# Embedding operand requested before the last group of ff1, two of four weight sums done by accumulating DMAs, another first and last stage

## The chip, the core and the metric

The kernel runs on one core of one Trainium2 chip. A core has a matrix engine (TensorE, here PE, with its weight loads as PEld), three elementwise engines (VectorE or DVE, ScalarE or ACT, GpSimd or POOL), a sync engine (SP), and 16 DMA engines that the queues of SP, ACT and POOL feed. The engines run their own instruction streams in order and wait for one another through semaphores. The metric is the device time of one execution in microseconds (us).

## The reference

A trunk of two layers on x of 512 frames by 1024 features, float32. Each layer has three parts, and a last norm follows:

```python
h  = rmsnorm(x, g1);  z = h @ W_in + b_in        # mLSTM q k v o i f, retention q k v g, two gates
x += (sig(gA) * (A @ W_bA) + sig(gB) * (B @ W_bB)) @ W_out    # A: mLSTM, B: retention, chunks of 64
x += relu(rmsnorm(x, g2) @ W1 + b1)**2 @ W2 + b2              # ff1 to 4096 features, ff2 back
x += sigmoid(rmsnorm(x, g3) @ W_pg) * (p[i] @ W_pe)           # per-layer embedding, p of 256 features
# after the last layer: out = rmsnorm(x, gf)
```

## The kernel before, in words

**Layout.** Everything is feature-major: x is a tile of 128 partitions x 8 tiles of features x 512 frames. Products are of float32 accuracy, made of three matmuls in the engine's rounded format (fp32r): each operand is split into a high part and the rest, and a product is hi·hi + hi·lo + lo·hi (`mm3`, lines 296 to 298; in pairs 338 to 340). ACT writes the high part (line 231), DVE subtracts it for the low one (line 232).

**Weights** come as blocks of 128 x 1024 (512 KB) in the order of use (`wstream`). `fill_raws` (line 250) keeps up to four raw blocks on their way on SP's queue; `prep_next` takes the next block, splits it into `wh` and `wl`; `ready(k)` prepares all up to the k-th piece, two units ahead of their use (`LOOK`). A T8 unit is one block for 24 matmuls over 512 columns. IF is the first unit of a layer (the mLSTM's gates, tile `l0if`).

**Norms.** `Norm.operand` writes gain times x, split (`l0n1h` on ACT, line 390; `l0n1l` on DVE, line 391); `square` makes the squares (ACT line 403, POOL line 401) and sums them over the feature tiles on POOL (line 409), all but the last one, which stays apart (`tail`). `finish` sums over partitions on PE with a matrix of ones, two matmuls for each 128 frames (`ss`, lines 416 and 417), POOL takes the root (`rc`), and `spread` puts the result on all partitions (`rp`, lines 434 and 435; `rb`, line 437). The scale is applied only behind the next matmul, so operands need not wait for it.

**ff1 and ff2.** Unit f(b,p) is two T8 tiles, evacuated and split into the hidden tiles `hh`, `hl`. ff2 is computed in groups of four pairs o(b,p), p = 0 to 3, by one level of the Winograd form of Strassen's product: 7 products of 12 matmuls over 256 columns instead of 8. Pair (b,p) adds into tiles 2p and 2p+1 of x on DVE (line 950). Its weights are four pieces out of two blocks r1 and r2: B11, t1 (a sum in r1), t2 (in r2) and t3 (a tile `t`), four half-block additions on DVE in all (lines 269, 270, 273, 277). The order of work is f(0,0..3), then for b = 0 to 2: f(b+1,0), o(b,0..3), f(b+1,1..3); then the matmuls of p[i] @ W_pe (two units PE, operand `pth`/`ptl` from `pT`, result `l0pe`), then the last group o(3,0..3), in which the tiles of the third norm (`n3.tile`) are made as x becomes final; then the gate tiles `pg` with n3's `finish` and `spread`.

**Tail.** The last four gate tiles are computed in halves of 256 frames, so that the last norm has two halves, n40 and n41; `final` multiplies x by gain and scale (three tiles on POOL, line 1050, five on DVE, line 1052) and sends it out (line 1054).

**What sets the order.** The code is written in program order, but the framework's scheduler decides at build time the order of instructions on each engine; on the chip each engine runs its own list in order. Names below are those of the first layer with l0, of the second with l1.

Of the kernel before, what the change touches and what calls it, by code (L numbers as in the profile page):

```python
# [33 lines left out]
F32 = mybir.dt.float32  # L34
# [15 lines left out]
LOOK = 2  # L50
RAWS = 4
PIECES = 3
PAD = 16
# [129 lines left out]
def build(ctx, tc, ins, out):  # L183
# [52 lines left out]
    for n, u in enumerate(units):  # L236
        if u[0] == "PAIR":
            order += [(n, x) for x in PIECE]
            loads += [(n, 0), (n, 1)]
        else:  # L240
            order.append((n, 0))
            loads.append((n, 0))
    place = {x: k for k, x in enumerate(order)}
# [3 lines left out]
    def fill_raws(most=RAWS):  # L247
        while at["load"] < len(loads) and sum(k[1] != "t" for k in raws) < most:
            raws[loads[at["load"]]] = r = wpool.tile([P, UN], F32, name=f"wr{at['load']}", tag="wr", bufs=RAWS)
            nc.sync.dma_start(r, ins["wstream"][at["load"]])  # L250
            at["load"] += 1

    def prep_next():
# [7 lines left out]
        if x in PIECE:  # L261
# [3 lines left out]
            if x == "B11":  # L265
                src, out_ = r2[:, c0], piece(cur["xw"], "b", Q)
            elif x == "t1":
                raws[n, "t"] = t = cur["xw"].tile([P, UN], F32, name=f"t{n}", tag="t")
                ve.tensor_tensor(t[:, c0], r1[:, c0], r2[:, c1], OP.add)
                ve.tensor_tensor(r1[:, c0], r1[:, c0], r2[:, c0], OP.add)  # L270
# [98 lines left out]
    class Norm:  # L369
# [23 lines left out]
        def square(self, k, x, pool=False):  # L393
            w = self.n * P
            x = x[:, self.s]
            if self.sum is None:
                sq = opool.tile([P, T], F32, name=f"{self.name}sum", tag="ssum" + self.half)[:, :w]
# [6 lines left out]
            if self.sum is None:  # L404
                self.sum = sq
            elif k == KT - 1:
                self.tail = sq
# [3 lines left out]
        def finish(self):  # L411
            n = self.name
            o = ps(f"{n}ss")
            for j in range(self.n):
                s = slice(j * P, (j + 1) * P)
                te.matmul(o[:, 2 * j:2 * j + 2], self.sum[:, s], ones[:, 0:2], start=True, stop=False)
                te.matmul(o[:, 2 * j:2 * j + 2], self.tail[:, s], ones[:, 0:2], start=False, stop=True)
# [6 lines left out]
        def spread(self):  # L424
# [11 lines left out]
            self.b = opool.tile([P, T], F32, name=f"{n}rb", tag="rb" + self.half)[:, :w]  # L436
# [175 lines left out]
    fill_raws(2)  # L612
    for k in range(0, KT, 2):
        nc.sync.dma_start(x[:, k:k + 2, :], ins["xT"][k:k + 2].rearrange("k p t -> p k t"))
    for k in range(KT):
        n1.operand(k, x[:, k, :])
    fill_raws()
    for k in range(KT):
        n1.square(k, x[:, k, :], k < 5)
# [3 lines left out]
    for i in range(L):  # L623
# [30 lines left out]
        for k in range(KT):  # L654
            s = slice(k * P, (k + 1) * P)
            mm3(og, wh[:, s], wl[:, s], xa[0][k], xa[1][k], k == 0, k == KT - 1)

# [280 lines left out]

        def ff2(b, p):
            def make(n):  # L940
# [11 lines left out]
                def done(x_, o):  # L952
# [8 lines left out]
                    elif x_ == "P4":  # L961
                        add(0, o, OP.add)
                        if b == 3:
                            for c in (2 * p, 2 * p + 1):
                                n3.tile(c, x[:, c, :])
# [7 lines left out]
        for kind, b, p in first:  # L973
# [3 lines left out]
            if group:  # L977
                run_pairs(group)
                group = []
# [208 lines left out]
```

## Time and profile before

| | us |
|---|---|
| three runs | 2444.41, 2439.2, 2441.95 |
| median | 2441.95 |
| profiled execution | 2438.42 |
| its span, first to last instruction | 2436.7 |
| mean granted TensorE clock | 0.993 |

The page's instruction count is 30731. The rows of a timeline read: start, duration, engine, line, operation, output <- inputs, shapes, number, and in brackets the engine's idle time before it and what ended it. In a list of waits, a row is the waiting instruction <- what it waited for: us in total, times, longest. A row that groups instructions gives shortest/median/longest in ns and the first and last start. A row of DMA issues gives queue, number, size and the median us from issue to landing.

In 40 equal slices of the span, the page has PE in tenths busy and the DMA engines' throughput:

```profile
PE   8999999999999999998999999999999999999997
...
GB/s 165 93 89 77 83 104 87 86 85 132 78 121 130 113 104 87 104 113 72 132 90 89 91 83 95 95 95 82 92 120 87 122 134 90 113 104 96 95 87 44
```

PE is at nine tenths or more nearly throughout, and lower at both ends.

### The profile page before, as it was taken

To read this page: it belongs to the slowest core of one execution; us is meant where nothing else is said; L and a number is where in the kernel's file an instruction comes from. 1 tells how busy PE (TensorE), PEld (TensorE's weight loads), DVE (VectorE), ACT (ScalarE), POOL (GpSimd) and SP (SyncE) were. 2 spreads that over 40 slices of the span, in tenths; PEclk is the share of its full clock that TensorE was granted. 3 is DMA by queue.
4 is the path that set the end of the run, shared out by engine and by line. 5 is a ranking of instruction groups with operands and counts; after the bars stand their busy time and mean duration, and the time that the engine had idled before them with its cause. 6 is when DMAs were issued, how large, how long until landed. Compare 5 with 4: busy or idle time off the path is not lost.

```text
span 2436.7 us, 30731 instructions
## 1 busy us (share of the span) xinstructions
PE 2390.5 (98%) x12220; PEld 2040.2 (84%) x12220; DVE 1574.1 (65%) x2403; ACT 1042.2 (43%) x1420; POOL 142.1 (6%) x213
## 2 busy tenths in 40 slices
PE   8999999999999999998999999999999999999997
PEld 6888888888888899898888888888888888998786
DVE  7867536663555678777778665466635547788675
ACT  4746323332333545544446552233333335445443
POOL 4100000000001000000201000000000010000012
PEclk9999999999999999999999999999999999999998
DMA  4222232223234332332322222222232342332221
GB/s 165 93 89 77 83 104 87 86 85 132 78 121 130 113 104 87 104 113 72 132 90 89 91 83 95 95 95 82 92 120 87 122 134 90 113 104 96 95 87 44
DMA packets 74417, 241.41 MB, mean 99 GB/s; under 512 B 8089, under 2 KB 10521, under 8 KB 74273
## 3 DMA queue, kind: packets, MB, share of 16 engines
q1 hardware_dynamic: 64336, 221.49, 27.3%
q10 hardware_dynamic: 9936, 17.96, 2.4%
q8 instruction: 96, 1.57, 0.3%
q14 instruction: 49, 0.39, 0.0%
HBM read 231.02 MB, written 8.39 MB: 98 GB/s over the span
## 4 chain that ended last, share of the span: by engine, by line
PE 95%; DVE 3%; ACT 1%; issue 1%; POOL 0%; DVEq 0%; ACTq 0%; POOLq 0%
PE l0f L296 2%; PE l1f L296 2%; PE l1f L297 2%; PE l0f L297 2%; PE l0f L298 2%; PE l1f L298 2%; PE l1br L297 1%; PE l1br L296 1%; PE l0br L298 1%; PE l0br L297 1%; PE l0br L296 1%; PE l1br L298 1%; PE l1bgm L296 1%; PE l0bgm L296 1%; PE l0wo L297 1%
## 5 line engine op out<-in xcount | busy, mean ns | idle before, releaser
L231 ACT ACTIVATE wh<-wr 128x1024 fp32r<-128x1024 f32 x342 | 361.7, 1059 | 851.8 <-issue 161.4
L232 DVE TENSOR_TENSOR wl<-wr,wh 128x1024 fp32r<-128x1024 f32 x342 | 419.1, 1227 | 216.0 <-ACT wh L231 215.7
L231 ACT ACTIVATE wh_t<-wr 128x1024 fp32r<-128x1024 f32 x64 | 66.9, 1058 | 84.6 <-DVE wr L270 53.6
L296 PE MATMUL l0f<-l0n2h,wh 128*128 128x512 f32 x256 | 99.8, 390 | 0.0
L296 PE MATMUL l1f<-l1n2h,wh 128*128 128x512 f32 x256 | 99.8, 390 | 0.0
L298 PE MATMUL l1f<-l1n2h,wl 128*128 128x512 f32 x256 | 99.7, 389 | 0.0
L298 PE MATMUL l0f<-l0n2h,wl 128*128 128x512 f32 x256 | 99.7, 389 | 0.0
L297 PE MATMUL l1f<-l1n2l,wh 128*128 128x512 f32 x256 | 99.7, 389 | 0.0
L297 PE MATMUL l0f<-l0n2l,wh 128*128 128x512 f32 x256 | 99.6, 389 | 0.0
L232 DVE TENSOR_TENSOR wl_t<-wr,wh_t 128x1024 fp32r<-128x1024 f32 x64 | 77.1, 1218 | 19.4 <-ACT wh_t L231 19.2
L231 ACT ACTIVATE wh_t<-t 128x1024 fp32r<-128x1024 f32 x32 | 33.9, 1061 | 58.6 <-DVE t L277 14.2
L298 PEld LDWEIGHTS l0f<-l0n2h,wl 128*128 128x128 f32 x256 | 48.1, 188 | 10.2
L298 PEld LDWEIGHTS l1f<-l1n2h,wl 128*128 128x128 f32 x256 | 48.1, 188 | 10.1
L297 PEld LDWEIGHTS l0f<-l0n2l,wh 128*128 128x128 f32 x256 | 48.1, 188 | 9.8
L297 PEld LDWEIGHTS l1f<-l1n2l,wh 128*128 128x128 f32 x256 | 48.1, 188 | 9.7
L296 PEld LDWEIGHTS l1f<-l1n2h,wh 128*128 128x128 f32 x256 | 48.1, 188 | 9.7
L296 PEld LDWEIGHTS l0f<-l0n2h,wh 128*128 128x128 f32 x256 | 48.1, 188 | 9.6
L232 DVE TENSOR_TENSOR wl_t<-t,wh_t 128x1024 fp32r<-128x1024 f32 x32 | 39.1, 1222 | 7.6 <-ACT wh_t L231 7.6
L231 ACT ACTIVATE wh_B<-wr 128x512 fp32r<-128x512 f32 x32 | 20.0, 626 | 24.6 <-issue 8.8
L409 POOL TENSOR_TENSOR l0n3sum<-l0n3sum,l0n3sq 128x512 f32<-128x512 f32 x6 | 9.4, 1572 | 348.9 <-issue 319.3
L409 POOL TENSOR_TENSOR l1n3sum<-l1n3sum,l1n3sq 128x512 f32<-128x512 f32 x6 | 8.9, 1487 | 349.3 <-ACT l1n3sum L403 319.7
L297 PE MATMUL l0pg<-l0n3l,wh 128*128 128x512 f32 x64 | 25.0, 393 | 0.2 <-DVE l0n3l L391 0.2
(3117 smaller groups left out, 7581.7 us busy)
## 6 DMA issues: line engine op xcount, KB each, us to landing
wr<-wstream SPq DMA_DIRECT2D x406, 512.0 KB, 3.3
x<-xT SPq DMA_DIRECT2D x4, 512.0 KB, 7.2
br_spill<-l0brs ACTq DMA_DIRECT2D x8, 256.0 KB, 2.0
l0brl<-br_spill ACTq DMA_DIRECT2D x8, 256.0 KB, 2.7
l0xr<-xT ACTq DMA_DIRECT2D x8, 256.0 KB, 2.7
x_spill<-l0x ACTq DMA_DIRECT2D x8, 256.0 KB, 2.2
br_spill<-l1brs ACTq DMA_DIRECT2D x8, 256.0 KB, 2.0
l1brl<-br_spill ACTq DMA_DIRECT2D x8, 256.0 KB, 2.7
```

Source lines behind the costliest of these rows:

```text
L231: ac.activation(hi_ap, src, AF.Copy)
L232: ve.tensor_sub(lo_ap, src, hi_ap.bitcast(F32))
L296: te.matmul(o, sh, mh, start=first, stop=False)
L297: te.matmul(o, sh, ml, start=False, stop=False)
L298: te.matmul(o, sl, mh, start=False, stop=last)
L409: gp.tensor_tensor(self.sum, self.sum, sq, OP.add)
```

## The change

1. **Start.** 20 matmuls of ones on PE into an unused tile; one weight block is requested ahead of x, not two; x comes as eight transfers of 256 KB, not four of 512 KB; the first weight split stands ahead of the norm's operands; the eight squares are all on ACT, behind IF's matmuls.
2. **Pairs.** Two of the four half-block sums are made by DMA: POOL's queue brings the first half of `t` and then adds the other block's half to it, and adds half a block to r1 as soon as r1 has been requested. For 32 pairs these are 96 transfers of 256 KB. Lines 269 and 270 go, lines 273 and 277 stay.
3. **Norms over all 512 frames.** DVE adds the last square to the sum, and PE takes one matmul for each 128 frames instead of two.
4. **Embedding operand.** Its transfer and split stand ahead of f(3,1), not behind f(3,3).
5. **n3's tiles in the last group.** Tiles 2p-2 and 2p-1 are made at products P6 and P7 of pair p, for p = 1 to 3, and tiles 6 and 7 at P4 of the last pair. Before, tiles 2p and 2p+1 came at P4 of pair p.
6. **Tail.** ACT multiplies by the gain tile by tile; `final` is one DVE product over four tiles (or two) with its own output transfer; POOL has no part in it. The half-size norm tiles are allocated at half size, the software DMA scratch is larger, and the padding constant is 32.

```diff
 LOOK = 2
+WARM = 20
 RAWS = 4
 PIECES = 3
-PAD = 16
+PAD = 32
 LAST = 4
...
             loads.append((n, 0))
+    first_block = {n: b for b, (n, k) in reversed(list(enumerate(loads)))}
     place = {x: k for k, x in enumerate(order)}
...
         while at["load"] < len(loads) and sum(k[1] != "t" for k in raws) < most:
-            raws[loads[at["load"]]] = r = wpool.tile([P, UN], F32, name=f"wr{at['load']}", tag="wr", bufs=RAWS)
+            n, k = loads[at["load"]]
+            raws[n, k] = r = wpool.tile([P, UN], F32, name=f"wr{at['load']}", tag="wr", bufs=RAWS)
             nc.sync.dma_start(r, ins["wstream"][at["load"]])
+            if units[n][0] == "PAIR" and k == 0:
+                gp.dma_start(r[:, 0:Q], ins["wstream"][at["load"] + 1][:, 0:Q], accum_op=OP.add)
             at["load"] += 1
...
             if x == "B11":
+                raws[n, "t"] = t = cur["xw"].tile([P, UN], F32, name=f"t{n}", tag="t")
+                b = first_block[n]
+                gp.dma_start(t[:, c0], ins["wstream"][b][:, c0])
+                gp.dma_start(t[:, c0], ins["wstream"][b + 1][:, c1], accum_op=OP.add)
                 src, out_ = r2[:, c0], piece(cur["xw"], "b", Q)
             elif x == "t1":
-                raws[n, "t"] = t = cur["xw"].tile([P, UN], F32, name=f"t{n}", tag="t")
-                ve.tensor_tensor(t[:, c0], r1[:, c0], r2[:, c1], OP.add)
-                ve.tensor_tensor(r1[:, c0], r1[:, c0], r2[:, c0], OP.add)
                 src, out_ = r1, piece(wpool, "w")
...
             if self.sum is None:
-                sq = opool.tile([P, T], F32, name=f"{self.name}sum", tag="ssum" + self.half)[:, :w]
+                sq = opool.tile([P, w if self.half else T], F32, name=f"{self.name}sum", tag="ssum" + self.half)[:, :w]
             else:
...
                 self.sum = sq
+            elif k == KT - 1 and self.n < NT:
+                self.tail = sq
             elif k == KT - 1:
-                self.tail = sq
+                ve.tensor_tensor(self.sum, self.sum, sq, OP.add)
             else:
...
                 s = slice(j * P, (j + 1) * P)
-                te.matmul(o[:, 2 * j:2 * j + 2], self.sum[:, s], ones[:, 0:2], start=True, stop=False)
-                te.matmul(o[:, 2 * j:2 * j + 2], self.tail[:, s], ones[:, 0:2], start=False, stop=True)
+                te.matmul(o[:, 2 * j:2 * j + 2], self.sum[:, s], ones[:, 0:2], start=True, stop=self.n == NT)
+                if self.n < NT:
+                    te.matmul(o[:, 2 * j:2 * j + 2], self.tail[:, s], ones[:, 0:2], start=False, stop=True)
             ms = cols.tile([P, NT], F32, name=f"{n}ms", tag="ms")[:, 0:self.n]
...
             te.matmul(o[:, :w], ones_r, dl, start=False, stop=True)
-            self.b = opool.tile([P, T], F32, name=f"{n}rb", tag="rb" + self.half)[:, :w]
+            self.b = opool.tile([P, w if self.half else T], F32, name=f"{n}rb", tag="rb" + self.half)[:, :w]
             ac.activation(self.b, o[:, :w], AF.Copy)
...
     n1 = Norm("l0n1", 0, "g1", acts(xa_pool, "l0n1"))
-    fill_raws(2)
-    for k in range(0, KT, 2):
-        nc.sync.dma_start(x[:, k:k + 2, :], ins["xT"][k:k + 2].rearrange("k p t -> p k t"))
+    warm = ps("warm")
+    for _ in range(WARM):
+        te.matmul(warm[:, 0:P], ones, ones, start=True, stop=True)
+    fill_raws(1)
+    for k in range(KT):
+        nc.sync.dma_start(x[:, k, :], ins["xT"][k])
+    ready(0)
     for k in range(KT):
         n1.operand(k, x[:, k, :])
-    fill_raws()
-    for k in range(KT):
-        n1.square(k, x[:, k, :], k < 5)
     nc.sync.dma_start(ident, ins["ident"])
...
             mm3(og, wh[:, s], wl[:, s], xa[0][k], xa[1][k], k == 0, k == KT - 1)
+        if i == 0:
+            for k in range(KT):
+                n1.square(k, x[:, k, :])
...
+        def tile3(c):
+            n3.tile(c, x[:, c, :])
         def ff2(b, p):
...
                         add(0, o, OP.add)
-                        if b == 3:
-                            for c in (2 * p, 2 * p + 1):
-                                n3.tile(c, x[:, c, :])
+                        if b == 3 and p == 3:
+                            tile3(6)
+                            tile3(7)
+                    if b == 3 and p and x_ in ("P6", "P7"):
+                        tile3(2 * p - 2 + (x_ == "P7"))
...
                 group = []
+            if (b, p) == (3, 1):
+                pth, ptl = [cur["ff"].tile([P, 2, T], F32R, name=f"l{i}pt{a}", tag=f"h{a}", bufs=5) for a in "hl"]
+                for k in range(2):
+                    t = tmp(f"l{i}ptr{k}")
+                    nc.scalar.dma_start(t, ins["pT"][i, k])
+                    split(t, pth[:, k, :], ptl[:, k, :])
             ff1(b, p)
...
         pe = n3_pool.tile([P, KT, T], F32, name=f"l{i}pe", tag="pe")
-        pth, ptl = [cur["ff"].tile([P, 2, T], F32R, name=f"l{i}pt{a}", tag=f"h{a}", bufs=5) for a in "hl"]
-        for k in range(2):
-            t = tmp(f"l{i}ptr{k}")
-            nc.scalar.dma_start(t[:, :T], ins["pT"][i, k])
-            split(t[:, :T], pth[:, k, :], ptl[:, k, :])
         for u in range(2):
...
-    def final(n):
-        for c in range(KT):
-            if c < 3:
-                gp.tensor_tensor(x[:, c, n.s], x[:, c, n.s], n.b, OP.mult)
-            else:
-                ve.scalar_tensor_tensor(x[:, c, n.s], x[:, c, n.s], n.col(c), n.b, OP.mult, OP.mult)
-        for c0, c1 in ((3, 6), (0, 2), (6, 8), (2, 3)):
-            nc.sync.dma_start(out[c0:c1, :, n.s].rearrange("c p t -> p c t"), x[:, c0:c1, n.s])
-    for c in range(3):
+    def final(n, c0, c1):
+        v = x[:, c0:c1, n.s]
+        ve.tensor_tensor(v, v, n.b.rearrange("p (a t) -> p a t", a=1).to_broadcast([P, c1 - c0, n.n * P]), OP.mult)
+        nc.sync.dma_start(out[c0:c1, :, n.s].rearrange("c p t -> p c t"), v)
+    for c in range(KT - LAST):
         ac.activation(x[:, c, :], x[:, c, :], AF.Copy, scale=nn[0].col(c))
...
             pe_evac(o, c, n.s, [n])
+            ac.activation(x[:, c, n.s], x[:, c, n.s], AF.Copy, scale=n.col(c))
             if a == 1 and c == KT - LAST:
                 nn[0].finish()
-            if a == 1 and c == KT - LAST + 1:
-                nn[0].spread()
-                final(nn[0])
+            elif a == 1 and c < KT - 1:
+                if c == KT - LAST + 1:
+                    nn[0].spread()
+                final(nn[0], 4 * (c - KT + LAST - 1), 4 * (c - KT + LAST))
     nn[1].finish()
     nn[1].spread()
-    final(nn[1])
+    for c0, c1 in ((0, 4), (4, 6), (6, 8)):
+        final(nn[1], c0, c1)
     cur["tmp"].release()
...
     }
-    nc = bacc.Bacc("TRN2", target_bir_lowering=False, num_devices=1, dynamic_dma_scratch_size=64)
+    nc = bacc.Bacc("TRN2", target_bir_lowering=False, num_devices=1, dynamic_dma_scratch_size=2048)
     aps = {n: nc.dram_tensor(n, v.shape, mybir.dt.from_np(v.dtype), kind="ExternalInput").ap()
```

On **ACT**, at the end of ff1 in layer 0 (`l0f33st` is the evacuation of f(3,3), `l0hh` its operand's high part, `wh_t` and `wh_0` high parts of weights), before:

```order
L923 ACTIVATE l0f33st<-l0f33st,bc 128x512
L924 ACTIVATE l0f33st<-l0f33st 128x512
L231 ACTIVATE l0hh_8988<-l0f33st 128x768
L231 ACTIVATE l0pth<-l0ptr_9089 128x512
L231 ACTIVATE l0pth<-l0ptr_9093 128x512
L231 ACTIVATE l0hh_8988<-l0f33st 128x1024
L999 ACTIVATE l0pe<-l0pe_9103 128x512
```

and the place of the same two splits after:

```order
L232 ACTIVATE wh_t_8764<-t_8682 128x1024
L232 ACTIVATE wh_0_8807<-wr_8680 128x1024
L232 ACTIVATE wh_0_8839<-wr_8797 128x1024
L232 ACTIVATE l0pth<-l0ptr_8871 128x512
L232 ACTIVATE l0pth<-l0ptr_8875 128x512
L232 ACTIVATE wh_0_8912<-wr_8799 128x1024
L937 ACTIVATE l0f31st<-l0f31st,bc 128x512
```

The splits `l0pth` moved from inside f(3,3)'s evacuation to a place ahead of f(3,1)'s.

On **POOL**, in the last ff2 group of layer 0 (`l0n3sum` is the running sum of squares of the third norm), before:

```order
L422 TENSOR_TENSOR l0n2rc<-l0n2ms,nhalf 128x4
L409 TENSOR_TENSOR l0n3sum<-l0n3sum,l0n3sq_9318 128x512
L409 TENSOR_TENSOR l0n3sum<-l0n3sum,l0n3sq_9442 128x512
L409 TENSOR_TENSOR l0n3sum<-l0n3sum,l0n3sq_9447 128x512
L409 TENSOR_TENSOR l0n3sum<-l0n3sum,l0n3sq_9571 128x512
```

and after, where `t_9264`, `t_9384` and `t_9512` are those of pairs 1, 2 and 3:

```order
L274 DMA t_9264<-wstream 128x512
L275 DMA t_9264<-wstream 128x512
L256 DMA wr_9259<-wstream 128x512
L256 DMA wr_9379<-wstream 128x512
L418 TENSOR_TENSOR l0n3sum<-l0n3sum,l0n3sq_9445 128x512
L274 DMA t_9384<-wstream 128x512
L275 DMA t_9384<-wstream 128x512
L418 TENSOR_TENSOR l0n3sum<-l0n3sum,l0n3sq_9538 128x512
L274 DMA t_9512<-wstream 128x512
L418 TENSOR_TENSOR l0n3sum<-l0n3sum,l0n3sq_9574 128x512
L275 DMA t_9512<-wstream 128x512
L418 TENSOR_TENSOR l0n3sum<-l0n3sum,l0n3sq_9666 128x512
```

POOL's queue, which held only the sums here, now carries the transfers of the pairs between them, in one order.

On **ACT** at the start of the program (`x_90` is x), before:

```order
L231 ACTIVATE wh_0_184<-wr_113 128x1024
L231 ACTIVATE wh_0_190<-wr_115 128x1024
L390 ACTIVATE l0n1h_97<-x_90,bc 128x512
L390 ACTIVATE l0n1h_99<-x_90,bc 128x512
L390 ACTIVATE l0n1h_101<-x_90,bc 128x512
```

and after, from the last operand on:

```order
L397 ACTIVATE l0n1h_111<-x_90,bc 128x512
L410 ACTIVATE l0n1sum<-x_90 128x512
L232 ACTIVATE wh_0_193<-wr_144 128x1024
L232 ACTIVATE wh_0_199<-wr_146 128x1024
L410 ACTIVATE l0n1sq_230<-x_90 128x512
L410 ACTIVATE l0n1sq_233<-x_90 128x512
```

The second weight split moved behind the eight operands, and the squares follow it on this engine.

## The prediction

> **What bounds the kernel now.** I read the page's busy shares and its chain first, then the list of what PE waited for, then windows around those waits.
>
> ```profile
> PE 2390.5 (98%) x12220; PEld 2040.2 (84%) x12220; DVE 1574.1 (65%) x2403; ACT 1042.2 (43%) x1420; POOL 142.1 (6%) x213
> PE 95%; DVE 3%; ACT 1%; issue 1%; POOL 0%; DVEq 0%; ACTq 0%; POOLq 0%
> ```
>
> TensorE (PE) is busy 98% of the span and carries 95% of the chain. The change leaves nearly all of its matmuls as they are, so a gain can come only from its idle time, from stretches at a lower clock, and from the few matmuls that go. Where PE is idle, the waits say, in us (total, times, longest):
>
> ```profile
> PE l0if L296 <- ACT l0n1h L390: 8.4, 1, 8.4
> PE l1n41ss L417 <- ACT l1n41sq L403: 5.1, 1, 5.1
> PE l0pe L296 <- ACT l0pth L231: 4.2, 1, 4.2
> PE l1pe L296 <- ACT l1pth L231: 4.2, 1, 4.2
> ...
> PE l0o33a L338 <- DVE l0x L950: 2.0, 1, 2.0
> PE l1o33a L338 <- DVE l1x L950: 2.0, 1, 2.0
> PE l1o32a L338 <- DVE l1x L950: 1.9, 1, 1.9
> PE l0o32a L338 <- DVE l0x L950: 1.9, 1, 1.9
> ...
> PE l1o31c L338 <- DVE l1x L950: 0.9, 1, 0.9
> ...
> PE l0o31c L338 <- DVE l0x L950: 0.7, 1, 0.7
> ```
>
> Four places: the start (l0if), the embedding operand (l0pe, l1pe), the last ff2 group (o31 to o33, in both layers) and the tail (n41). The windows of layer 0 show them beside undisturbed stretches; after the engines' busy time stand the granted clock, the DMA share and GB/s.
>
> ```profile
> core 0: us, PE busy (x) PEld busy (x) DVE busy (x) ACT busy (x) POOL busy (x), PEclk, DMA share, GB/s
> 1076.00:1100.00 24.00, 24.00 (x107) 19.89 (x106) 16.79 (x23) 13.78 (x18) 0.00 (x0) 1.00 0.29 91
> 1101.40:1105.70 4.30, 0.18 (x1) 0.00 (x0) 4.07 (x5) 4.24 (x7) 0.00 (x0) 0.83 0.03 9
> 1105.70:1119.20 13.50, 13.47 (x48) 10.61 (x49) 5.90 (x9) 6.69 (x10) 0.00 (x0) 0.80 0.22 75
> 1020.00:1072.00 52.00, 51.95 (x392) 49.59 (x391) 43.47 (x70) 22.33 (x26) 0.00 (x0) 1.00 0.33 112
> 1131.00:1144.00 13.00, 12.25 (x102) 11.93 (x101) 11.83 (x19) 5.58 (x8) 1.81 (x1) 1.00 0.19 57
> 1144.00:1158.00 14.00, 11.98 (x88) 11.51 (x87) 12.69 (x18) 6.30 (x9) 3.40 (x2) 0.88 0.24 85
> ```
>
> The first row, part of ff1, gives the price of a matmul over 512 columns: 24.00 / 107 = 0.224 us. The fourth is a middle ff2 group: PE never idle, DVE busy 43.47 of 52.
>
> **The change, term by term.** The sum is made against the profiled execution, 2438.4 us (its span 2436.7 and 1.7 around it); the median of the runs is 2441.95, 3.5 more, and I add that at the end.
>
> **1. Start.** Views: the timeline of the first 20 us, and one group for DVE's price without POOL beside it.
>
> ```profile
> 4.92 1.06 ACT L231 ACTIVATE wh<-wr 128x1024 fp32r<-128x1024 f32 x1 [2.41 <-DMA wr<-wstream]
> 7.65 3.98 ACT L390 ACTIVATE l0n1h<-x,bc 128x512 fp32r<-128x512 f32 x6 [0.36 <-DMA x<-xT]
> 8.46 9.55 DVE L391 SCALAR_TENSOR_TENSOR l0n1l<-x,bc,l0n1h 128x512 fp32r<-128x512 f32 x8
> 12.94 0.63 PE L297 MATMUL l0if<-l0n1l,wh 128*128 128x512 f32 x1
> 13.37 0.63 PE L298 MATMUL l0if<-l0n1h,wl 128*128 128x512 f32 x1
> 18.41 0.39 PE L298 MATMUL l0if<-l0n1h,wl 128*128 128x512 f32 x1
> 26.58 2.64 POOL L409 TENSOR_TENSOR l0n1sum<-l0n1sum,l0n1sq 128x512 f32<-128x512 f32 x2
> L391 DVE SCALAR_TENSOR_TENSOR l0n3l<-l0x,bc,l0n3h x8: 745/1550/1835, 1133.0 to 1171.4; 128x512 fp32r<-128x512 f32 x8
> ```
>
> IF's matmuls end at 18.64, 0.23 after the last one's start. What ends last ahead of them is DVE's row of eight low halves: 9.55 / 8 = 1.19 us each beside POOL's squares, 0.745 at the least elsewhere. The change drops the second weight block ahead of x and the squares on POOL. The operands' high halves then follow the first split at 5.98 and end at 5.98 + 8 x 0.66 = 11.3; the low halves follow the one weight split (7.25) and end at 7.25 + 8 x 0.745 = 13.2; three last matmuls make IF end at 13.9. That is 4.7 earlier, if PE's clock is up. At the old start the matmuls stood 0.43 apart (12.94 to 13.37, five us after PE's first): 24 of them would take 10.3 us and, from about 7.3, end at 17.6, only 1 earlier. The 20 matmuls on ones decide that; PE is idle until 8.4 anyway, so they themselves cost nothing. Behind IF the sum of squares is next late: with ACT's next two weight splits ahead of them the squares run from 14.6, six POOL sums of 1.32 (2.64 / 2) with small work between end near 24.5 and DVE's last add near 25.3 (estimates), while PE, which had 29.31 - 18.64 = 10.7 us of matmuls between IF's end and this sum (term 3's rows), comes to it at 24.6: a wait of 0.7. I take **-4.2**, with n1's share of term 3 in it; range -6 to -1.
>
> The Trainium skill, "TensorE: Matmul & The Clock Gate", Part 1, has the clock return to full after about 3.4 us of sustained work. This trace still has 0.43 us five us after the first matmul, in a stretch with gaps; by the page the term is -4.2, by the row carried over to the new matmuls -1.
>
> **2. Embedding operand ahead of f31.** PE waits 4.3 us (the second window), since the transfer and the split of pT stand behind f33's evacuation on ACT. Then 48 matmuls take 13.5 us at a clock of 0.80; 48 x 0.224 = 10.8, so 2.7 are lost to the clock. Moved, the split is done 30 us earlier, and both go: 6.9 per layer. What takes its place: two ACT splits and two DVE subtractions at the end of a middle group, where ACT is busy 22.3 of 52 us and DVE 43.5, and no PE wait stands there. Next late is f33's evacuation, which P1 of the last group's pair 0 needs: the 4.24 us of ACT and 4.07 of DVE in the second window and some of the third are that evacuation, and it now has the 10.8 us of the pe matmuls above it. **-13.8** for both layers; -8.4 if the clock's part stays.
>
> **3. One matmul in place of two in the norms' sum.**
>
> ```profile
> 29.31 0.35 PE L416 MATMUL l0n1ss<-ones,l0n1sum 128*128 128x2 f32 x2
> ...
> 31.09 0.49 PE L296 MATMUL l0m0z<-l0n1h,wh 128*128 128x512 f32 x1
> ```
>
> 16 records in 31.09 - 29.31 = 1.78 us; half go, 0.89 per norm. Five norms beside l0n1: **-4.4**. The added DVE add stands on the way to the sum, about 0.7 to 1.4 (its 128x512 forms, next fence), and at n3 18 gate matmuls, 18 x 0.224 = 4.0 us of PE, stand behind the last tile in PE's order and cover it; at n2 there are fewer, which the upper end allows for. Range -5.3 to -3.
>
> **4. ff2 pairs.** Rows: DVE's sum that goes, then three splits of one middle group, and the shortest and longest landing of 256 KB.
>
> ```profile
> L269 DVE TENSOR_TENSOR t<-wr,wr x32: 677/684/1427, 842.4 to 2349.7; 128x512 f32<-128x512 f32 x32
> 1041.59 1.23 DVE L232 TENSOR_TENSOR wl_t<-t,wh_t 128x1024 fp32r<-128x1024 f32 x1 [0.56 <-ACT wh_t L231]
> 1050.97 1.06 ACT L231 ACTIVATE wh_t<-t 128x1024 fp32r<-128x1024 f32 x1 [1.42 <-PE l0o21a L339]
> 1060.79 1.06 ACT L231 ACTIVATE wh_t<-t 128x1024 fp32r<-128x1024 f32 x1 [2.64 <-PE l0o22a L339]
> br_spill<-l0brs ACTq DMA_DIRECT2D x8, 256.0 KB, 2.0
> l1m0bv<-bv SPq DMA_DIRECT2D x1, 256.0 KB, 3.6
> ```
>
> A pair takes 60.79 - 50.97 = 9.8 us; DVE loses 2 x 0.68 of its work in it. In groups 0 to 2 PE doesn't wait, so that is worth 0. In the last group PE's waits are 4.6 to 4.8 us per layer (2.0 + 1.9 + 0.7 or 0.9), and the clock of 0.88 costs 0.12 x 14 = 1.7 more: 6.4. DVE is busy 24.5 of 27 us there; without 2.7 of it, and with two norm tiles spread over P6 and P7 of the next pair, it still stands near the pitch of PE. I take half, **-6** for both layers; ends -13 (all) and +3 (the n3 sums on POOL hold back the transfers queued behind them).
>
> The two POOL transfers that build t run one behind the other. They may begin when the old t is split (1041.59 + 1.23 = 1042.8) and must land before ACT takes t at 1050.97: 8.1 us, about 7.4 without issue and hand-over (my estimate, one 0.7 us DVE add). DVE's slack of 8.5 in 52, 1.6 per pair, hides some 1.5 more: 8.9 before PE waits. No row shows an accumulating transfer. The nearest show 2.0 to 3.6; twice the longer, 7.2, is my upper end, since it reads what it writes. I take 3.6 and 2.7, 6.3 in all: **0**. On POOL nothing else is queued there but the next pairs' transfers, and in the last group the n3 sums.
>
> The Trainium skill, "DMA: Bandwidth & Descriptors", Anatomy of one DMA, gives 2.0 us plus bytes / 436e3 for this path: 2.6 for 256 KB, an estimate of 5.2 for two, with which the sum stays as it is. No run here shows it yet.
>
> **5. Tail.**
>
> ```profile
> 2419.67 3.56 DVE L1052 SCALAR_TENSOR_TENSOR l1x<-l1x,bc,l1n40rb 128x256 f32<-128x256 f32 x5 [0.45 <-ACT l1n40rb L437]
> 2429.08 3.57 DVE L1052 SCALAR_TENSOR_TENSOR l1x<-l1x,bc,l1n41rb 128x256 f32<-128x256 f32 x5 [1.09 <-ACT l1n41rb L437]
> ```
>
> Both stand on the chain. Two ops over four tiles at 1.23 (the 128x1024 subtraction above) replace the first five on DVE and three on POOL: 2.46 for 3.56, -1.1, so the second set begins 1.1 earlier; it takes 1.23 + 2 x 0.68 = 2.6 for 3.57, -1.0. The last transfer stays. **-2.1**, range -4 to -1.
>
> Sum: -4.2 - 13.8 - 4.4 - 6 - 2.1 = **-30.5**: 2407.9 on the profiled basis, **2411** on the median. With all ends at their best (-6, -13.8, -5.3, -13, -4) it is -42 (2400), at their worst (-1, -8.4, -3, +3, -1) -10.4 (2431).
>
> **Rivals.**
> - **Slower: the accumulating transfers are late.** Price: (time of two - 8.9) in pairs 2 and 3 of eight groups, 16 times. It eats the whole gain at 30.5 / 16 = 1.9, that is at 10.8 us for two, 5.4 each; at 7.2 each it is 16 x 5.5 = 88 slower, near 2499. Against: the landing rows stop at 3.6. For: nothing in the trace accumulates. Chance 0.18, of which 0.11 ends slower and 0.03 even.
> - **The last group keeps its waits** (DVE at the pitch, or n3 sums ahead of the transfers): -24.5, 2417. For: 24.5 of 27 us busy. Against: 1.4 less per pair. Chance 0.17.
> - **The start gives 1 or nothing** (clock down, or PE waits at n1's sum): 2415. Chance 0.10.
> - **The clock stays low around the pe matmuls, or P1 of the last group waits for f33**: -5.4 or so, 2416. Chance 0.05.
>
> **How the numbers follow.** The forecast has 0.50. Faster: 0.50 + 0.17 + 0.10 + 0.05 + 0.04 = 0.86; same 0.03; slower 0.11, with 0.2% (4.9 us) as about what a measurement can tell from no change. The range runs from 2398, the best ends less what medians scatter, to 2434, past all terms at their worst; only the first rival reaches further.
>
> **What would show it.** After: no PE wait for pth in either layer and the pe block near 10.8 us; IF ending near 14; n1ss, n2ss, n3ss at 8 records; the waits of o31 to o33 halved; no PE wait on wh_t or wl_t of t in groups 0 to 2; the last DVE op ending 2 us sooner behind the last matmul. I am wrong if POOL's transfers take over 4.4 us each, if ACT's split of t waits for a DMA, or if the last group's waits come back behind the n3 sums.

## The result, and the profile after

| | before | after |
|---|---|---|
| median, us (runs) | 2441.91 (2439.2 to 2444.41, 4) | 2462.56 (2459.47 to 2463.05, 4) |
| profiled execution, us | 2438.42 | 2462.41 |
| its span, us | 2436.7 | 2460.7 |

The ratio is 1.0082, with an interval of 1.0065 to 1.01: the changed kernel is some 20 us slower. The prediction, 2411 in a range of 2398 to 2434, is wrong, in its sign too.

From the page of the changed kernel, the engines' busy shares, the DMA queues with their share of the 16 engines' span, and the chain:

```profile
PE 2397.4 (97%) x12212; PEld 2048.5 (83%) x12212; DVE 1532.5 (62%) x2340; ACT 1048.8 (43%) x1434; POOL 197.8 (8%) x298
...
q1 hardware_dynamic: 64352, 221.49, 26.5%
q0 software_dynamic: 11776, 25.17, 5.3%
...
PE 86%; DMA 8%; DVE 3%; issue 2%; ACT 1%; POOL 0%; POOLq 0%; DVEq 0%; ACTq 0%; SPq 0%
```

DVE lost 41.6 us of work (1574.1 to 1532.5), as the change says, and 8% of the chain is now DMA, which had no share in it before. That is the first sign that the loss lies with transfers. The list of PE's waits, from its top:

```profile
PE l1n41ss L427 <- ACT l1n41sq L410: 3.9, 1, 3.9
PE l1o33a L345 <- DVE l1x L967: 2.9, 1, 2.9
PE l0o33a L345 <- DVE l0x L967: 2.8, 1, 2.8
PE l0o32a L345 <- DVE l0x L967: 2.7, 1, 2.7
PE l1o32a L345 <- DVE l1x L967: 2.7, 1, 2.7
PE l0o13c L345 <- DVE l0x L967: 2.6, 1, 2.6
PE l1o23c L345 <- DVE l1x L967: 2.5, 1, 2.5
```

The waits for the embedding operand and for the first norm are gone. In their place stand waits in all groups of pairs, o0x to o3x. They name DVE's additions to x, but DVE is in order and works less than before: something ahead of those additions is late. The waits of the other engines in the same kernel say what, in four rows of their list:

```profile
POOL t L275 <- DMA t<-wstream: 102.1, 30, 6.8
ACT wh_t L232 <- DMA t<-wstream: 99.8, 16, 9.5
POOL t L274 <- DVE wl_t L233: 84.2, 15, 9.0
...
DVE wl_t L233 <- ACT wh_t L232: 72.3, 46, 4.6
```

ACT stood 99.8 us in 16 places, 6.2 each, until a transfer into t had landed; DVE's subtraction waits for that split, and the additions to x stand behind it in DVE's queue. The four rows form a ring: POOL's first transfer waits for DVE to be done with the old t, the second for the first, ACT for the second, DVE for ACT. A wait of ACT's split of t for a DMA is one of the signs that the prediction named for being wrong.

The timeline of group 0 in layer 0, POOL's issues first and then ACT's splits of t:

```profile
870.64 0.86 POOL L256 DMA_DIRECT2D wr<-wstream  x1 [18.97 <-DVE wl_t L233]
871.22 0.86 POOL L274 DMA_DIRECT2D t<-wstream  x1
877.97 0.85 POOL L275 DMA_DIRECT2D t<-wstream  x1 [5.88 <-DMA t<-wstream]
884.98 0.57 POOL L274 DMA_DIRECT2D t<-wstream  x1 [6.16 <-DVE wl_t L233]
888.90 0.85 POOL L275 DMA_DIRECT2D t<-wstream  x1 [3.36 <-DMA t<-wstream]
```

```profile
867.39 1.06 ACT L232 ACTIVATE wh_t<-t 128x1024 fp32r<-128x1024 f32 x1 [1.13 <-PE l0o00a L346]
882.30 1.06 ACT L232 ACTIVATE wh_t<-t 128x1024 fp32r<-128x1024 f32 x1 [5.86 <-DMA t<-wstream]
895.11 1.06 ACT L232 ACTIVATE wh_t<-t 128x1024 fp32r<-128x1024 f32 x1 [7.35 <-DMA t<-wstream]
```

```profile
869.04 1.22 DVE L233 TENSOR_TENSOR wl_t<-t,wh_t 128x1024 fp32r<-128x1024 f32 x1
883.39 1.22 DVE L233 TENSOR_TENSOR wl_t<-t,wh_t 128x1024 fp32r<-128x1024 f32 x1 [3.63 <-ACT wh_t L232]
```

The third piece is DVE's subtractions, with whose end t is free: at 870.3 and 884.6. From there to the next split are 12.0 us in the first turn (to 882.30) and 10.5 in the second (to 895.11); before, 8.3 were enough for the first of these turns and 7.3 for the second (to the splits at 884.26 and 893.89 of the same group). The splits stand 14.9 and 12.8 us apart, against 9.8. In the first turn t's transfer is issued 0.6 us behind r1's accumulating one, and the second can follow only 6.75 us later; in the second turn, with nothing ahead, after 3.9. There are two such turns in each of the eight groups, for pairs 2 and 3: the 16 places of ACT's row.

**Where the time went.** Each row is the time from a stage's first matmul to the next one's, from the groups by tile of the three profiled executions, both layers together; the third column is the kernel of the first experiment.

| stage, us | before | after | e1_dve_sums |
|---|---|---|---|
| start to W_out of layer 0 | 761.6 | 756.2 | 756.6 |
| W_out to o00 of layer 0; n3 of layer 0 to o00 of layer 1 | 990.6 | 986.8 | 986.6 |
| ff2 groups 0 to 2 with ff1 beside them | 487.5 | 520.5 | 479.6 |
| pe matmuls | 27.8 | 22.0 | 22.0 |
| last groups | 105.1 | 112.8 | 99.8 |
| n3's sum of layer 1 to the end | 64.1 | 62.4 | 62.7 |
| span | 2436.7 | 2460.7 | 2407.3 |

Everything gains but the rows of the pairs: 33.0 lost in groups 0 to 2, in which the 7.9 that the third column gains there lie hidden, and 7.7 in the last groups. Against the third column, the pairs cost 40.9 and 13.0, 53.9 together.

Not all of that is idle time. PE's waits in the pairs add up to 46.3 us in the changed kernel and to 6.5 in the third column's. The granted clock fell too: over layer 1's groups 0 to 2 (2068.2 to 2329.5) it was 0.98, over the last groups 0.97 in layer 0 (1125.9 to 1180.9) and 0.91 in layer 1 (2340.5 to 2398.3). That is some 12 us; in the third column's kernel it was 1.00 in all of these stretches. The 39.8 us of waits and the 12 of clock make up nearly all of the 53.9; that the waits set off the fall of the clock is likely, but not shown.

### The profile page after: what moved, and what is told of

Its sections match the earlier page's. It is cut to its first block, busy times and chain, and to the rows that moved or that the text cites. A ratio compares the mean times of both kernels' runs of the same rounds, so it can differ in the third digit from the quotient of the medians.

```text
span 2460.7 us, 30966 instructions
## 1 busy us (share of the span) xinstructions
PE 2397.4 (97%) x12212; PEld 2048.5 (83%) x12212; DVE 1532.5 (62%) x2340; ACT 1048.8 (43%) x1434; POOL 197.8 (8%) x298
## 3 DMA queue, kind: packets, MB, share of 16 engines
q1 hardware_dynamic: 64352, 221.49, 26.5%
## 4 chain that ended last, share of the span: by engine, by line
PE 86%; DMA 8%; DVE 3%; issue 2%; ACT 1%; POOL 0%; POOLq 0%; DVEq 0%; ACTq 0%; SPq 0%
DMA t<-wstream 6%; PE l0f L303 2%; PE l1f L303 2%; PE l1f L304 2%; PE l0f L304 2%; PE l0f L305 2%; PE l1f L305 2%; PE l1br L304 1%; PE l1br L303 1%; PE l0br L305 1%; PE l0br L304 1%; PE l0br L303 1%; PE l1br L305 1%; DMA wr<-wstream 1%; ACT wh_t L232 1%
## 5 line engine op out<-in xcount | busy, mean ns | idle before, releaser
L303 PE MATMUL l1f<-l1n2h,wh 128*128 128x512 f32 x256 | 99.8, 390 | 0.0
L303 PE MATMUL l0f<-l0n2h,wh 128*128 128x512 f32 x256 | 99.8, 390 | 0.0
L232 ACT ACTIVATE wh_t<-t 128x1024 fp32r<-128x1024 f32 x32 | 33.8, 1056 | 106.8 <-DMA t<-wstream 99.8
L256 POOL DMA_DIRECT2D wr<-wstream x32 | 27.3, 852 | 380.8 <-DMA wr<-wstream 125.7
L275 POOL DMA_DIRECT2D t<-wstream x32 | 27.5, 858 | 102.1 <-DMA t<-wstream 102.1
L274 POOL DMA_DIRECT2D t<-wstream x32 | 20.1, 629 | 119.0 <-DVE wl_t L233 84.2
L232 ACT ACTIVATE wh_B<-wr 128x512 fp32r<-128x512 f32 x32 | 20.0, 626 | 14.4 <-PE l0o32a L346 2.8
```

The lines of the kernel that those rows point to most:

```text
L232: ac.activation(hi_ap, src, AF.Copy)
L256: gp.dma_start(r[:, 0:Q], ins["wstream"][at["load"] + 1][:, 0:Q], accum_op=OP.add)
L274: gp.dma_start(t[:, c0], ins["wstream"][b][:, c0])
L275: gp.dma_start(t[:, c0], ins["wstream"][b + 1][:, c1], accum_op=OP.add)
L303: te.matmul(o, sh, mh, start=first, stop=False)
```

## The experiments

Theory L: the two transfers into t, one behind the other, close a ring that is longer than a pair. Rivals: another part of the change makes the new waits; the 96 transfers are too many altogether; only the shared queue counts.

### e1_dve_sums: both sums back on DVE

```diff
-            if units[n][0] == "PAIR" and k == 0:
-                gp.dma_start(r[:, 0:Q], ins["wstream"][at["load"] + 1][:, 0:Q], accum_op=OP.add)
...
-                gp.dma_start(t[:, c0], ins["wstream"][b][:, c0])
-                gp.dma_start(t[:, c0], ins["wstream"][b + 1][:, c1], accum_op=OP.add)
...
             elif x == "t1":
+                ve.tensor_tensor(t[:, c0], r1[:, c0], r2[:, c1], OP.add)
+                ve.tensor_tensor(r1[:, c0], r1[:, c0], r2[:, c0], OP.add)
```

> The changed kernel with both half sums back on DVE and no transfer on POOL's queue; everything else of the change stays. Theory T (the sums by transfers cost some 42 us in groups 0 to 2 and some 8 to 14 in the last groups, and the other parts gain what was forecast): 2405 to 2418 us, PE waits of o0x to o2x gone. Rival U (another part of the change, such as the moved n3 tiles, the moved operand or the new order of the splits, brings the new waits): 2435 us or more, with the waits still there.

Measured: 2407.97 us (2406.62 to 2409.77), ratio to before 0.9861 (0.9841 to 0.988). So the rest of the change is worth some 33 us, and the transfers cost 54.6. It beats both kernels. PE's waits there, in the groups of pairs:

```profile
PE l0o32a L341 <- DVE l0x L963: 1.7, 1, 1.7
PE l1o32a L341 <- DVE l1x L963: 1.7, 1, 1.7
...
PE l0o33a L341 <- DVE l0x L963: 1.1, 1, 1.1
...
PE l1o33a L341 <- DVE l1x L963: 0.8, 1, 0.8
```

No wait over 0.2 us is left in groups 0 to 2, and the last groups are shorter than before although DVE does all its sums.

### e2_sums_alone: the transfers in the kernel before

```diff
+            if units[n][0] == "PAIR" and k == 0:
+                gp.dma_start(r[:, 0:Q], ins["wstream"][at["load"] + 1][:, 0:Q], accum_op=OP.add)
...
             if x == "B11":
+                raws[n, "t"] = t = cur["xw"].tile([P, UN], F32, name=f"t{n}", tag="t")
+                b = first_block[n]
+                gp.dma_start(t[:, c0], ins["wstream"][b][:, c0])
+                gp.dma_start(t[:, c0], ins["wstream"][b + 1][:, c1], accum_op=OP.add)
...
-                ve.tensor_tensor(t[:, c0], r1[:, c0], r2[:, c1], OP.add)
-                ve.tensor_tensor(r1[:, c0], r1[:, c0], r2[:, c0], OP.add)
```

> The kernel before with the two POOL sums alone (and the half-size norm tiles and the larger scratch that they need room for). Theory T: 42 us in groups 0 to 2 and 8 to 14 in the last groups: 2485 to 2500 us. Rival U: the sums alone cost little, 2440 to 2460.

Measured: 2482.99 us (2480.09 to 2487.43), ratio 1.017 (1.015 to 1.0191): 41.5 us, a little under the expected range. Groups 0 to 2 lose 35.5 by their first matmuls, the last ones 6.7. The sums by transfers cost by themselves, without any other part of the change; in the changed kernel they cost 12 to 13 more (by the spans and by the medians): 40.9 instead of 35.5 in groups 0 to 2, and 13.0 instead of 6.7 in the last groups, which had become shorter there without them.

### e3_operand_alone: only the moved operand

```diff
+            if (b, p) == (3, 1):
+                pth, ptl = [cur["ff"].tile([P, 2, T], F32R, name=f"l{i}pt{a}", tag=f"h{a}", bufs=5) for a in "hl"]
+                for k in range(2):
+                    t = tmp(f"l{i}ptr{k}")
+                    nc.scalar.dma_start(t[:, :T], ins["pT"][i, k])
+                    split(t[:, :T], pth[:, k, :], ptl[:, k, :])
             ff1(b, p)
```

(The same six lines go from their place behind f(3,3).)

> The kernel before with the embedding operand's transfer and split moved ahead of f(3,1), and nothing else. If the idle time and the clock's part both go, 13 to 14 us less than before: 2427 to 2429 us. If only the idle time goes: 2433. If the last group's first product waits for f33's evacuation instead: 2437 or more.

Measured: 2425.72 us (2425.04 to 2427.29), ratio 0.993 (0.9913 to 0.9948). The time is a little below the expected range. The profiled span fell from 2436.7 to 2423.6, by 13.1; the ratio's interval is 13 to 21 us. Idle time and clock part both go: the pe matmuls of layer 0 ran from 1101.8 to 1112.3, all at full pace, in the groups by tile:

```profile
L296 PE MATMUL l0pe<-l0pth,wh x16: 394/394/398, 1101.8 to 1112.1; 128*128 128x512 f32 x16
L297 PE MATMUL l0pe<-l0ptl,wh x16: 388/388/397, 1102.0 to 1112.3; 128*128 128x512 f32 x16
```

Before, the longest of the sixteen in the first of these rows took 797 ns; now 398.

### e4_t_only: r1's sum on DVE, t's on POOL

```diff
-            if units[n][0] == "PAIR" and k == 0:
-                gp.dma_start(r[:, 0:Q], ins["wstream"][at["load"] + 1][:, 0:Q], accum_op=OP.add)
...
             elif x == "t1":
+                ve.tensor_tensor(r1[:, c0], r1[:, c0], r2[:, c0], OP.add)
```

> The changed kernel with t still made by two POOL transfers, but r1's sum back on DVE, so that no transfer of r1 stands ahead of t's on POOL's queue. Theory Q (most of the delay is the shared queue: t's first transfer took 6.4 us behind r1's): two at about 4.1 each fit into about 9, 2412 to 2430 us. Rival S (two in series are too long by themselves): 2440 us or more, ACT still waiting for t.

Measured: 2450.35 us (2449.4 to 2452.23), ratio 1.0037 (1.0024 to 1.0051). Taking r1's transfers away gives 12.2 us back, and the other 42 stay with two transfers in series: rival S holds. How much of the 12.2 is the shared queue isn't shown: in e8_one_copy below, where r1's transfers have POOL's queue to themselves, some 7 are still lost. The trace prices the two kinds apart, here the plain first transfer and then the accumulating second one (count and issue time, then issue to landing):

```profile
L271 POOL DMA_DIRECT2D t<-wstream x32: 561/561/792, 798.2 to 2360.7; - x32
...
DMA to landing us min/median/max: 2.8/2.9/3.7
```

```profile
DMA to landing us min/median/max: 3.6/5.6/7.5
```

256 KB each: 2.9 us plain, 5.6 accumulating, with no transfer of r1 in the queue. In the changed kernel the same two lines have 3.2 (at most 7.3) and 4.7 (at most 8.0).

### e5_first_on_SP: the plain transfer on SP's queue

```diff
-                gp.dma_start(t[:, c0], ins["wstream"][b][:, c0])
+                nc.sync.dma_start(t[:, c0], ins["wstream"][b][:, c0])
```

> The changed kernel with t's plain first transfer on SP's queue; the accumulating ones stay on POOL. Theory S (the length of the chain counts, and one in two becomes a transfer of about 3 us): 8 to 9 us from t's release, 2415 to 2440 us. Theory Q (queueing behind r1's accumulating transfer counts, which now meets the second one): 2445 us or more.

Measured: 2438.09 us (2434.66 to 2441.7, 10 runs), ratio 0.9985 (0.9976 to 0.9995): 24.5 us less than the changed kernel, and 30 more than e1_dve_sums. The copy lands in 2.6 us there (2.5 to 3.7); the accumulating one behind it still takes 4.4 at the median (3.6 to 7.9). A shorter ring makes a smaller loss, as theory S has it; Q falls as the main cause.

### e6_two_buffers: the same transfers, two buffers

```diff
-                raws[n, "t"] = t = cur["xw"].tile([P, UN], F32, name=f"t{n}", tag="t")
+                raws[n, "t"] = t = cur["xw"].tile([P, Q], F32, name=f"t{n}", tag="t", bufs=2)
...
-                gp.dma_start(t[:, c0], ins["wstream"][b][:, c0])
-                gp.dma_start(t[:, c0], ins["wstream"][b + 1][:, c1], accum_op=OP.add)
+                gp.dma_start(t, ins["wstream"][b][:, c0])
+                gp.dma_start(t, ins["wstream"][b + 1][:, c1], accum_op=OP.add)
...
-                ve.tensor_tensor(src[:, c1], r2[:, c0], r1[:, c1], OP.add)
+                u = cur["xw"].tile([P, Q], F32, name=f"tb{n}", tag="tb")
+                ve.tensor_tensor(u, r2[:, c0], r1[:, c1], OP.add)
...
+                split(src, *[a[:, c0] for a in out_])
+                src, halves = u, out_
+                out_ = [a[:, c1] for a in out_]
```

(And a scratch of 1024 instead of 2048.)

> The changed kernel with t's transferred half in a tile of its own with two buffers (the half that DVE adds in another tile, so t is split in two halves; a scratch of 1024 bytes makes room). The same 96 transfers run. Theory L (the delay is a loop: t is free, two transfers, split, t is free, 11 to 14 us against a pair's 9.8): the second buffer opens the loop, 2408 to 2425 us. Rival W (96 transfers are too much for the queue or the DMA engines, or slow down other work): 2445 us or more.

Measured: 2429.21 us (2427.01 to 2432.31), ratio 0.9945 (0.9926 to 0.9964): 33 us come back with all 96 transfers still running, so W falls as the main cause. It ended a little above L's range. The waits of ACT's splits of t:

```profile
  DMA t<-wstream: 10.4, 2
```

10.4 us in 2 places, against 99.8 in 16. What is left, 21 us above e1_dve_sums, is for the most part not ACT's wait for t. In groups 0 to 2 PE waits 14.0 us, and the granted clock is 0.98 over layer 0's (855.7 to 1108.7), some 5 us. PE's largest wait there is the first group's o01a, 5.2 us, and ACT waits 15.4 us in 5 places for r1's transfers, which the build had put behind t's in POOL's order. The twice-split t also adds an instruction per pair on ACT and on DVE. How the waits divide between these wasn't tried.

### e7_old_n3_place: the norm's tiles back at P4

```diff
-                        if b == 3 and p == 3:
-                            tile3(6)
-                            tile3(7)
-                    if b == 3 and p and x_ in ("P6", "P7"):
-                        tile3(2 * p - 2 + (x_ == "P7"))
+                        if b == 3:
+                            tile3(2 * p)
+                            tile3(2 * p + 1)
```

(On top of e1_dve_sums.)

> The kernel with both sums on DVE (e1_dve_sums) and the third norm's tiles back at P4 of each pair. Theory N (the placement alone relieves the last group, 2.7 us per layer in the trace of e1_dve_sums): 2412 to 2415 us. Rival: the last group is bound by DVE's pair sums, and the placement gives nothing: 2406 to 2410.

Measured: 2417.44 us (2413.89 to 2420.66), ratio 0.9895 (0.9874 to 0.9916), against 2407.97 with the new places; that is above theory N's range and far from its rival's. The medians say 9.5; the profiled spans, 2412.2 and 2407.3, say 4.9, and the last groups in them are 3.2 and 3.6 longer. PE's waits of before are back: 2.0 at o33a and 1.9 at o32a in both layers. So the placement relieves the last group by itself, by the 6.8 of the last groups. In the spans 1.4 of it are lost again behind n3's sum of layer 1 (62.7 with the new places, 61.3 here; the clock at the end of this document); why the medians differ by more isn't settled.

### e8_one_copy: a plain copy on SP and one sum on DVE, r1 on POOL

```diff
-                gp.dma_start(t[:, c0], ins["wstream"][b][:, c0])
-                gp.dma_start(t[:, c0], ins["wstream"][b + 1][:, c1], accum_op=OP.add)
+                nc.sync.dma_start(t[:, c0], ins["wstream"][b][:, c0])
...
             elif x == "t1":
+                t = raws[n, "t"]
+                ve.tensor_tensor(t[:, c0], t[:, c0], r2[:, c1], OP.add)
```

> The changed kernel with t's first half copied by a plain transfer on SP's queue (2.6 us to landing in e5_first_on_SP) and the other block's half added by DVE; r1's sum stays an accumulating transfer on POOL. One DVE sum per pair less than in e1_dve_sums. Theory L: copy and DVE sum take 3.5 to 4.5 us of the 8.1, the loop is shorter than a pair, and r1's transfer has four raw buffers: 2403 to 2412 us. Rival: r1's accumulating transfers delay t1 and the loads by themselves: 2418 or more.

Measured: 2414.68 us (2412.53 to 2417.45), ratio 0.9881 (0.9861 to 0.9902). It lies between the two theories. Without the accumulating transfer in t the ring is open; r1's transfers, with four raw buffers, and the copy together still cost some 7 us against e1_dve_sums (8.5 by the spans; the intervals of the ratios overlap a little), and the DVE sum saved in every pair doesn't make up for it.

### e9_no_warm: the start without the matmuls of ones

```diff
-WARM = 20
+WARM = 0
```

(On top of e1_dve_sums.)

> The kernel with both sums on DVE (e1_dve_sums) without the 20 matmuls of ones at the start. Theory C (without them the matmuls of IF run 0.43 us apart, as at the old start): IF ends near 17 instead of 13.9, 2410 to 2412 us. Rival (IF is bound by DVE's low halves or the transfers of x either way): within 1 us of e1_dve_sums, with IF ending near 14.

Measured: 2409.46 us (2409.03 to 2409.86), ratio 0.9864 (0.9848 to 0.9881): not to be told from e1_dve_sums in the time. The timeline shows theory C's mechanism nevertheless, IF's matmuls, which end near 16.4 and not at 13.9:

```profile
9.20 0.63 PE L299 MATMUL l0if<-l0n1h,wh 128*128 128x512 f32 x1
9.63 0.63 PE L300 MATMUL l0if<-l0n1l,wh 128*128 128x512 f32 x1
...
14.82 0.39 PE L301 MATMUL l0if<-l0n1h,wl 128*128 128x512 f32 x1
15.05 0.39 PE L299 MATMUL l0if<-l0n1h,wh 128*128 128x512 f32 x1
```

0.43 us apart until 13.9, 0.23 from 14.6 on, and n1's sum starts at 27.3, not at 25.2 as in e1_dve_sums. The 20 matmuls are worth 2.1 us at that place; most of it comes back in the last stage, which is 1.5 shorter than in e1_dve_sums (the clock at the end of this document).

### e10_plain_second: two plain transfers

```diff
-                gp.dma_start(t[:, c0], ins["wstream"][b + 1][:, c1], accum_op=OP.add)
+                gp.dma_start(t[:, c0], ins["wstream"][b + 1][:, c1])
```

(On top of e4_t_only; the sum in t's first half is left out.)

> The kernel of e4_t_only (both of t's transfers on POOL, r1's sum on DVE), its second transfer plain instead of accumulating, in the same order; the sum in t is left out, so t's first half holds only the second block's values. Theory A (the accumulating transfer is the slow one: 5.6 us median to landing against 2.9 for the plain one in the trace of e4_t_only): two plain ones take under 7 us, the loop is shorter than a pair, 2405 to 2420 us. Rival P (the second one is slow because it meets the next pair's weight blocks, whatever its kind): 2440 to 2452.

Measured: 2427.36 us (2427.3 to 2431.97), ratio 0.9942 (0.9925 to 0.9958), between the two: 23 us less than e4_t_only, 19 more than e1_dve_sums. The second transfer's landing:

```profile
DMA to landing us min/median/max: 3.0/4.4/6.2
```

Of its 5.6 us, 1.2 at the median come from accumulating. The other 4.4 are 1.5 longer than the 2.9 of the first one. A likely reason is that the second one meets the next pair's weight blocks: in e4_t_only three of them are issued between 885.4 and 888.2. These are the windows of e4_t_only in which a first transfer and then a second one run:

```profile
core 0: us, PE busy (x) PEld busy (x) DVE busy (x) ACT busy (x) POOL busy (x), PEclk, DMA share, GB/s
...
882.70:885.90 3.20, 2.73 (x21) 2.56 (x22) 3.00 (x7) 1.50 (x2) 0.55 (x2) 1.00 0.24 87
885.90:893.10 7.20, 6.66 (x59) 6.46 (x57) 3.49 (x6) 0.51 (x1) 0.84 (x1) 1.00 0.79 240
```

The DMA engines are busy 0.24 of the first window and 0.79 of the second; in the turns before and after it is 0.65 and 0.78, and 0.40 and 0.64. The DMA packets in the trace of e10_plain_second say the same of all 32 second transfers. The four beside which less than 200 KB of weights moved took 2.7 to 3.0 us from issue to their last packet, the 14 with more than 800 KB 4.0 to 5.4. This is a correlation: that weight blocks moved out of the way would shorten the transfer wasn't tried.

## Why the prediction was wrong, by its steps

1. **Start, -4.2: right.** The time to W_out fell by 5.4; the term's own figures (a sum at 25.3 and not at 29.31, and n1's 0.89) come to 4.9. IF ended at 13.9, as worked out, but it was held by the matmuls of ones (they ended at 8.4, so they weren't free: in e9_no_warm the first operand is there at 6.9) and then by PE itself, not by DVE's low halves, which ended at 12.7; the sum came at 24.9 without a wait. The Trainium skill, "TensorE: Matmul & The Clock Gate", Part 1, has the clock back after at least one busy window of about 3.4 us, with windows that run freely. The matmuls of ones fit that: they took from 1.06 to about 5 in e1_dve_sums and from 1.07 to about 7 in the changed kernel until more of them came in a microsecond (7 and then 11; 7 and then 10). In e9_no_warm it took from 6.9 to about 14, with a gap of 0.51 in front of the second matmul. The profile's clock column reads 1.00 from the start, but the trace's first clock record, a full one, stands only at 4.8, 7.1 and 14.4 in these three runs. So 3.4 us as a fixed time was too short, and the row was the better guide.
2. **Embedding operand, -13.8: right.** 13.1 in e3_operand_alone's span, and the same in the stage table: in e1_dve_sums 7.9 less ahead of the pe matmuls and 5.8 in them, 13.7.
3. **Norms' sums, -4.4: right.** The two long stages between lost 3.8 of it, one sum in the last stage is the fifth.
4. **Pairs: the step that failed.** "I take 3.6 and 2.7, 6.3 in all: 0". From the release of t to the next split the two take 9.8 to 12.6 us in the 16 places, 11.25 at the mean. In the same turns of e1_dve_sums, where ACT waits for no transfer into t, it is 8.2 and 7.4 in groups 0 to 2. Added up over the twelve turns of these groups, the changed kernel takes 41.0 us more, and the groups lost 40.9: nothing hid any of it. In the four turns of the last groups it takes 8.1 more, and they lost 13.0, with some 7 of clock in them.
   Two sizes were wrong, the transfers' time and what the kernel bears. The prediction took the 8.1 us of one turn, a pair 2, for all of them; the trace of before has some 7.3 for pair 3, and 10.6 to 11.7 in the last groups. It then added a slack of 1.5: 8.9 for the transfers alone, which is 9.6 from release to split. With that, the first rival's formula gives 16 x 1.65 = 26, less than the gain of 30.5, so by it the kernel would still have been faster. Without the slack its break-even from release to split is 8.1 + 1.9 = 10.0, and 11.25 is past it. So the mechanism stood among the rivals and its number was mis-sized.
   The nearest rows were plain transfers on ACT's and SP's queues. What they left out, in the order in which the runs took it away: r1's transfers (12 us, e4_t_only), accumulating in t (23 us, e10_plain_second; 1.2 of the 5.6 us to landing), and 19 us left with two plain transfers, of which the second lands in 4.4 and not 2.9, most likely beside the weight blocks. Another order gives other shares: the first transfer on SP's queue alone gives 24.5 back (e5_first_on_SP), a second buffer 33 (e6_two_buffers). The Trainium skill, "DMA: Bandwidth & Descriptors", Anatomy of one DMA, has a fit that comes to 2.6 for 256 KB, an estimate. The first transfer of e4_t_only, at 2.9, is near it; the plain second one (4.4) and the accumulating one (5.6) are not, and of accumulating ones that section says nothing.
5. **Last groups, -6: undone.** They lost 7.7: PE's waits there rose from 10.4 to 13.6, and the clock took some 5 more than before. In both layers POOL's sum for the third norm (1152.96 to 1154.25 in layer 0) also stands ahead of pair 3's first transfer, which could have been issued at 1152.9 and was at 1154.21; the prediction's second rival named that. Without the transfers the last groups gain 5.3, the size forecast. Of the two reasons that the prediction gave, DVE's saved sums are not in it (e1_dve_sums keeps them on DVE), the places of n3's tiles are (e7_old_n3_place). The prediction also counted 1.7 of clock in both layers; before, the clock was 0.97 over layer 0's last group and 1.00 over layer 1's.
6. **Tail, -2.1: right.** From the last gate matmul to the span's end 18.3 before (2418.4 to 2436.7), 16.4 after (2444.3 to 2460.7).

The terms 1, 2, 3, 5 and 6 add up to -30.5, and e1_dve_sums, which holds just these, is 29.4 faster by its span. That they agree so well is in part luck: the start gives 0.8 more than its term there, and the last stage 1.6 less. Nearly all of the error is in the one price. Its rival's chance was set too low, too: for an operation that no row shows, with bounds of 2.0 and 7.2 around a tolerance of some 4 each, 0.18 for the far side had no row behind it.

## What to carry to other kernels

Work moved from an engine to a DMA is free only if its latency fits into the time for which its buffer is free: find the ring (buffer free, transfers, reader, buffer free), add up its longest case with every transfer ahead on the same queue, and compare it with the pitch of the loop. A price from rows of plain transfers doesn't carry over to accumulating ones beside a busy stream (2.9 and 5.6 us here); measure it first. And taking work off an engine that nobody waits for brought nothing here: of this change the parts that pay are the earlier request, the shorter chains at both ends and the places of the norm's tiles, and e1_dve_sums, which keeps them and leaves the sums on DVE, is the fastest version (0.9861 of before).

## What was not expected of the hardware

An accumulating transfer costs the DMA engines more than its bytes. The rows of a queue give packets, MB and the share of the 16 engines' span. On the page of e8_one_copy, where all transfers of the software queue accumulate, its row is

```profile
q0 software_dynamic: 4608, 8.39, 2.2%
```

and on that of e10_plain_second, where none does,

```profile
q0 software_dynamic: 5120, 16.78, 2.3%
```

That is 0.26% for a MB against 0.14%, about 1.9 times. The weight queue of the changed kernel holds 0.12% for a MB (26.5% for 221.49 MB).

In the last gate tiles (`pl`) the granted clock fell in the second half to 0.88 in the changed kernel and 0.89 in e1_dve_sums (27.9 us from the first to the last matmul). It stayed at 1.00 before and in e9_no_warm (26.4), although e9_no_warm has the same instructions there as e1_dve_sums. The cause of these 1.5 us is open.
